# Attention steps of a two-layer decoder trunk in a fixed issue order on four engines

## The chip, the cores and the metric

One core of a Trainium2 chip runs the whole program. The metric is the device time of one execution in microseconds (us). Engine names are those of the profile: PE is TensorE (PEld its weight loads), DVE is VectorE, ACT is ScalarE, POOL is GpSimd, SP is SyncE, which issues nearly all DMAs.

## What is computed

The program is a decoder trunk of two layers on 512 tokens of width 1024, all in fp32. What matters here is the cross-attention of layer 1, a sliding window of 128 keys with ALiBi slopes and one sink logit per head:

```python
def mixer_b(xn, w_q, sinks, w_o, kblk, vblk):
    q = (xn @ w_q).reshape(B, nb, BLOCK, N_KV_HEADS, GQA_GROUP, HEAD_DIM)
    scores = jnp.einsum('bnikgd,bnjkd->bnkgij', q, kblk) * (HEAD_DIM ** -0.5)
    ...
    scores = scores - slopes[:, :, None, None] * dist
    scores = jnp.where(valid[None, :, None, None], scores, -jnp.inf)
    m = jnp.maximum(jnp.max(scores, axis=-1, keepdims=True), sink)
    e = jnp.exp(scores - m)
    probs = e / (jnp.sum(e, axis=-1, keepdims=True) + jnp.exp(sink - m))
    out = jnp.einsum('bnkgij,bnjkd->bnikgd', probs, vblk)
    return out.reshape(B, S, N_Q_HEADS * HEAD_DIM) @ w_o
```

There are 16 heads in 4 groups that share keys and values, and 4 blocks of 128 tokens. Around it stand norms, gated MLPs and dense products, which the change leaves alone.

## The kernel before, in words

Every fp32 product is made of three matmuls in a faster format (L191): weights and inputs are split into a high part (a cast) and a low part (the difference). A weight "unit" of 128x1024 is loaded by SP into one of a few raw buffers (`load`), cast by ACT into `wh` (L170) and subtracted by DVE into `wl` (L171); `pump` does this for the next units, `take` and `chunk` hand them to the matmuls. In the attention only two raw buffers are in use, so a load waits until the `wl` of the unit two before is done.

The attention runs 16 steps, one for each pair of group g and block n (i = 4g + n). A step i works on three attention blocks at different ages:

- `scores(i)`, L707: eight PE matmuls into the two PSUM banks `sc`.
- `logits(i)`: DVE merges the two key blocks (L720, not for n = 0), scales and adds ALiBi into `prs` (L721), for n = 0 masks instead (L723), and takes the row minimum `low` (L728).
- `exps(i)`, L736: four ACT exponentials, one a head, whose sums go to `sm`.
- `weights(i)`: DVE's reciprocal of `sm` (L742), then POOL multiplies `prs` by it (L743).
- `turn(i-1)`, L750: four PE transposes of the step before into the single PSUM bank `tr`; `turned_hi` casts it on ACT (L765, `ph` or `pp`), `turned_lo` takes the low part on DVE (L771) and POOL masks both (L774).
- `mix(i-2)`, L788: PE's product with the values into the single PSUM bank `pv`; `low_rows` copies half of it on ACT (L794, `pb`); `outputs` adds the halves on DVE (L806), casts on ACT (L810, `oh`) and subtracts on POOL (L813, `ol`).

Between these, PE does "fill" work, five pieces of three 512-column matmuls a step: 48 pieces of `project` (the queries of groups 1 to 3) and then pieces of `merge` (the output projection). A finished query half goes through `queries` (a cast on ACT, L259, a subtraction on DVE, L260, four DMAs of SP, about 0.6 us of issue each). A finished merge is added to h on DVE (L687). After every fourth step DVE rescales `alibi` (L726).

The order of the instructions on each engine is not the order of the code: a scheduler of the framework chooses it when the program is built, within the data dependencies. Each engine then runs its list strictly in that order.

Of the kernel before, what the change touches and what calls it, by code (L numbers as in the profile page):

```python
# [1 line left out]

# [50 lines left out]
def tile_yoco(ctx: ExitStack, tc: tile.TileContext, t, out: bass.AP, out_b: bass.AP):  # L53
# [18 lines left out]
    def psum2(name):  # L72
        return mmp.tile([P, 2, S], F32, tag="sc", name=name)


    units = []

# [257 lines left out]
    def slope(hd):  # L335
        return 2.0 ** (-8.0 * (hd + 1) / HEADS)
# [317 lines left out]
    for c in range(NC):  # L654
        ps = psum(f"vv{c}")
        mm3t(ps[:, :256], xkv, parts, 0, 256, c)
        vf.append(tp.tile([P, 256], F32, tag="rstd", name=f"vf{c}"))
        nc.scalar.activation(vf[c], ps[:, :256], AF.Copy, scale=rt[:, c : c + 1])
        halves(vt[c // 2][:, c % 2], vf[c])
        if c:  # L660
            d = tp.tile([P, 256], F32, tag="acc", name=f"vdf{c}")
            nc.gpsimd.tensor_sub(d, vf[c - 1], vf[c])
            halves(vd[:, c - 1], d)

    box = {}
# [12 lines left out]
    def merge(m, k0, k1, first, last, ps=None):  # L678

        c, half = m // 2, k0 // 4  # L680
        if (c, half) not in box:
            box[c, half] = chunk(256, 4, ahead=0)
        if first:
            box[f"o{m}"] = psum(f"o{m}_{half}", "mm") if ps is None else ps
        mm3(box[f"o{m}"], box[c, half][k0 % 4 : (k1 - 1) % 4 + 1], o2[k0:k1], m % 2 * P, first=first, last=last)
        if last:
            nc.vector.tensor_add(h[m], h[m], box[f"o{m}"])  # L687

    steps = [(g, n) for g in range(GROUPS) for n in range(NC)]
    live = {}  # L690
# [23 lines left out]
    def logits(i, o):  # L714

        g, n = steps[i]
        pr = prs[:, i % 2]
        cur = o[:, :, P:]
        if n:
            nc.vector.copy_predicated(cur, above.bitcast(U32).unsqueeze(1).to_broadcast([P, GQ, P]), o[:, :, :P])  # L720
        nc.vector.scalar_tensor_tensor(pr[:, :, :P], cur, rq[:, n : n + 1], alibi, op0=ALU.mult, op1=ALU.add)  # L721
# [3 lines left out]
        if n == NC - 1 and g + 1 < GROUPS:  # L725
            nc.vector.tensor_scalar_mul(alibi, alibi, slope(GQ - 1))  # L726
        low = at.tile([P, GQ], F32, tag="low", bufs=2, name=f"low{i}")
        nc.vector.tensor_reduce(low, pr, axis=mybir.AxisListType.X, op=ALU.min)  # L728
        sm = at.tile([P, GQ], F32, tag="sm", bufs=2, name=f"sm{i}")
        live[i] = [pr, low, sm]  # L730

    def exps(i, es):

        pr, low, sm = live[i]
        for e in es:
            nc.scalar.activation(pr[:, e, :], pr[:, e, :], AF.Exp, bias=low[:, e : e + 1], scale=-1.0,  # L736
                                 accum_out=sm[:, e : e + 1])

    def weights(i):

        pr, low, sm = live[i]
        nc.vector.reciprocal(sm, sm)  # L742
        nc.gpsimd.tensor_mul(pr[:, :, :P], pr[:, :, :P], sm.unsqueeze(2).to_broadcast([P, GQ, P]))  # L743

    def turn(i):
# [20 lines left out]

    def turned_lo(i, tr):

        n = steps[i][1]
        ph, pl, mh, ml = live[i]  # L770
        nc.vector.tensor_sub(pl, tr, ph.bitcast(F32))  # L771
        if n:
            for a, b in ((ph, mh), (pl, ml)):
                nc.gpsimd.affine_select(out=b, in_=a.bitcast(F32), pattern=[[0, GQ], [-1, P]], compare_op=ALU.is_gt,  # L774
                                        fill=0.0, base=0, channel_multiplier=1)

    def mix(i):

# [18 lines left out]
    def outputs(i, ps, b):  # L797

        g, n = steps[i]
        if n == 0:  # L800
            for m in (2 * g, 2 * g + 1):
                o2.append([ap.tile([P, S], F32R, tag=f"a{x}{m}", name=f"o{x}{m}") for x in "hl"])
        x, y = (a.rearrange("p (b e t) -> p b e t", b=2, e=2) for a in (ps, b))
        of = y[:, :, 0, :]
        for e in range(2):
            nc.vector.tensor_add(of[sides[e]], x[:HD, :, e, :], y[:HD, :, e, :])  # L806
        cols = slice(n * P, (n + 1) * P)
        for a in range(2):
            oh, ol = o2[2 * g + a]
            nc.scalar.copy(oh[:, cols], of[:, a, :])  # L810
        for a in range(2):
            oh, ol = o2[2 * g + a]
            (nc.gpsimd if i < last - 1 else nc.vector).tensor_sub(ol[:, cols], of[:, a, :], oh[:, cols].bitcast(F32))  # L813

    last = len(steps)
    work = [(project, u) for u in range(48)]
# [12 lines left out]
    sinks(0)  # L829
    for i in range(last):  # L830
        o = scores(i)
        logits(i, o)
        pump(state["next"] + WBUFS - 1)
        fill(i, 0, 3)
        if i:
            tr = turn(i - 1)
        exps(i, (0,))
        if i:
            turned_hi(i - 1, tr)
        exps(i, (1,))  # L840
        fill(i, 3, 4)
        if i >= 2:
            pv = mix(i - 2)
            pb = low_rows(i - 2, pv)
        exps(i, (2, 3))
        if i:
            turned_lo(i - 1, tr)
        if i >= 2:
            outputs(i - 2, pv, pb)
        fill(i, 4, None)  # L850
        weights(i)
        if i + 1 < last:
            sinks(i + 1)
    fill(last, 0, 2)
    tr = turn(last - 1)
    turned_hi(last - 1, tr)
    turned_lo(last - 1, tr)
    pv = mix(last - 2)
    outputs(last - 2, pv, low_rows(last - 2, pv))
    state["cap"] = len(units)  # L860
    load(held_back + 2)
    for m in (2, 3):
        merge(m, 4, 6, False, False)
    pv = mix(last - 1)
    outputs(last - 1, pv, low_rows(last - 1, pv))
    state["tags"], state["turn"] = list(range(RAWS)), 2
    load(held_back + 6)
    two = psum2("o5")
    merge(4, 4, 6, True, False, psum("o4_1", "tr"))
    merge(5, 4, 6, True, False, two[:, 0])  # L870
    piece, pef, pet = ple_in_both()
    nf = Norm("nf1", [(xp, "x", gain("norm_ffn", 1))])
    for m in range(KD):
# [209 lines left out]
```

## Time and profile before

| | us |
|---|---|
| median of three runs | 1145.34 |
| lowest and highest of them | 1145.27, 1147.95 |
| profiled execution, whole | 1146.59 |
| profiled execution, span from first to last instruction | 1144.9 |
| PE busy in the span | 1123.8 |
| PE waits between 593 and 701 us of the span | 5.9 |

The granted clock was 0.997 on average. A row of the timeline gives start and duration of an instruction, its engine and line, output<-inputs by the program's names, and in brackets how long the engine had sat idle and what ended that. In the tables of waits a row gives who waited for whom, the total, the number of times and the longest.

### The profile page before, as it was taken

The page shows a single profiled execution, that of the slowest core. Times are in us where ns is not written, and L with a number is a line of the kernel's source. Part 1 is how long each engine was busy: PE and PEld are TensorE (multiplying, and loading weights), DVE is VectorE, ACT ScalarE, POOL GpSimd, SP SyncE. Part 2 cuts the span into 40 slices and gives each one's busy share as a digit, 9 for nine tenths or more (in the row PEclk, how much of TensorE's full clock was granted, in tenths as well). Part 3 has the DMA queues.
Part 4 walks back from the last instruction along what each step waited for, and adds up shares of the span by engine and source line. Part 5 has one row for each costly group of instructions (what it writes and reads, how often), then busy time and mean ns, then how long its engine had stood idle before and what let it go on. Part 6 is the DMA issues. An engine that isn't in the chain of part 4 may idle for free.

```text
span 1144.9 us, 13730 instructions
## 1 busy us (share of the span) xinstructions
PE 1123.8 (98%) x5248; PEld 936.6 (82%) x5248; DVE 737.1 (64%) x983; ACT 509.7 (45%) x807; POOL 139.8 (12%) x169
## 2 busy tenths in 40 slices
PE   9999999999999999999998999999999999999996
PEld 7888888888888888888887778888888888888895
DVE  7356477763676367557867886687734774577656
ACT  6534344431343244445656666554423442344532
POOL 2100310000000000022225553200000000000232
PEclk9999999999999999999999999999999999999998
DMA  9322222322322333233063414433322323332202
GB/s 334 105 85 84 100 92 93 110 92 92 111 71 95 111 110 94 91 110 104 13 180 92 129 57 139 141 109 91 110 92 93 101 69 106 110 97 87 79 15 74
DMA packets 44690, 116.48 MB, mean 102 GB/s; under 512 B 4936, under 2 KB 16848, under 8 KB 44624
## 3 DMA queue, kind: packets, MB, share of 16 engines
q1 hardware_dynamic: 43504, 114.42, 31.8%
q10 hardware_dynamic: 1120, 1.18, 0.3%
q8 instruction: 41, 0.67, 0.2%
q14 instruction: 25, 0.20, 0.1%
HBM read 108.24 MB, written 2.11 MB: 96 GB/s over the span
## 4 chain that ended last, share of the span: by engine, by line
PE 89%; DVE 4%; ACT 2%; issue 2%; POOL 1%; DMA 1%; SPq 0%; POOLq 0%; ACTq 0%; DVEq 0%
PE up L197 14%; PE up L198 14%; PE up L199 14%; PE d L197 8%; PE d L199 8%; PE d L198 8%; PE gate L197 2%; PE gate L199 2%; PE gate L198 2%; PE u L199 1%; PE u L197 1%; PE u L198 1%; PE v L209 1%; PE v L208 1%; PE v L210 1%
## 5 line engine op out<-in xcount | busy, mean ns | idle before, releaser
L171 DVE TENSOR_TENSOR wl<-wraw,wh 128x1024 fp32r<-128x1024 f32 (+2 forms) x197 | 238.3, 1211 | 121.7 <-ACT wh L170 120.7
L170 ACT CAST wh<-wraw 128x1024 fp32r<-128x1024 f32 (+1 forms) x196 | 202.1, 1033 | 237.4 <-PE d L198 135.8
L197 PE MATMUL up<-nf00h,wh 128*128 128x512 f32 x352 | 137.1, 390 | 0.0
L197 PE MATMUL up<-nf10h,wh 128*128 128x512 f32 x352 | 137.0, 389 | 0.0
L199 PE MATMUL up<-nf00h,wl 128*128 128x512 f32 x352 | 137.0, 389 | 0.0
L199 PE MATMUL up<-nf10h,wl 128*128 128x512 f32 x352 | 136.9, 389 | 0.0
L198 PE MATMUL up<-nf10l,wh 128*128 128x512 f32 x352 | 136.9, 389 | 0.0
L198 PE MATMUL up<-nf00l,wh 128*128 128x512 f32 x352 | 136.9, 389 | 0.0
L197 PE MATMUL d<-ah,wh 128*128 128x512 f32 x352 | 136.9, 389 | 0.0
L198 PE MATMUL d<-al,wh 128*128 128x512 f32 x352 | 136.9, 389 | 0.0
L199 PE MATMUL d<-ah,wl 128*128 128x512 f32 x352 | 136.9, 389 | 0.0
L384 ACT ACTIVATE c<-hs,vec 128x512 f32<-128x512 f32 x88 | 71.7, 815 | 88.2 <-DVE hs L380 87.2
L385 DVE SCALAR_TENSOR_TENSOR c<-hs,vec,c 128x511 f32<-128x511 f32 x88 | 65.9, 749 | 37.4 <-ACT c L384 37.2
L358 DVE TENSOR_TENSOR h<-h,d 128x512 f32<-128x512 f32 x56 | 38.5, 687 | 69.0 <-PE d L199 69.0
L259 ACT CAST ah<-a 128x512 fp32r<-128x512 f32 x44 | 27.4, 622 | 113.5 <-DVE a L390 113.5
L199 PEld LDWEIGHTS up<-nf00h,wl 128*128 128x128 f32 x352 | 66.1, 188 | 13.9
L197 PEld LDWEIGHTS up<-nf10h,wh 128*128 128x128 f32 x352 | 66.1, 188 | 13.8
L199 PEld LDWEIGHTS d<-ah,wl 128*128 128x128 f32 x352 | 66.1, 188 | 13.8
L197 PEld LDWEIGHTS d<-ah,wh 128*128 128x128 f32 x352 | 66.1, 188 | 13.7
L198 PEld LDWEIGHTS up<-nf10l,wh 128*128 128x128 f32 x352 | 66.1, 188 | 13.7
L198 PEld LDWEIGHTS d<-al,wh 128*128 128x128 f32 x352 | 66.1, 188 | 13.7
L198 PEld LDWEIGHTS up<-nf00l,wh 128*128 128x128 f32 x352 | 66.1, 188 | 13.6
(314 smaller groups left out, 2031.1 us busy)
## 6 DMA issues: line engine op xcount, KB each, us to landing
wraw<-in_w_up SPq DMA_DIRECT2D x88, 512.0 KB, 3.5
wraw<-in_w_down SPq DMA_DIRECT2D x32, 512.0 KB, 3.6
wraw<-in_w_down SPq DMA_DIRECT2D x16, 384.0 KB, 3.2
wraw<-in_w_u SPq DMA_DIRECT2D x8, 512.0 KB, 5.7
wraw<-in_w_out SPq DMA_DIRECT2D x8, 512.0 KB, 3.5
wraw<-in_w_gate SPq DMA_DIRECT2D x8, 512.0 KB, 4.1
wraw<-in_w_q SPq DMA_DIRECT2D x8, 512.0 KB, 3.7
wraw<-in_w_o SPq DMA_DIRECT2D x8, 512.0 KB, 3.3
```

The source lines that it names most:

```text
L170: nc.scalar.copy(wh[:, :n], src)
L171: nc.vector.tensor_sub(wl[:, :n], src, wh[:, :n].bitcast(F32))
L197: nc.tensor.matmul(ps, wh[:, a:b], xh, start=st, stop=False)
L198: nc.tensor.matmul(ps, wh[:, a:b], xl, start=False, stop=False)
L199: nc.tensor.matmul(ps, wl[:, a:b], xh, start=False, stop=en)
L208: nc.tensor.matmul(ps, xh[:, s], wh[:, a:b], start=st, stop=False)
L209: nc.tensor.matmul(ps, xl[:, s], wh[:, a:b], start=False, stop=False)
L210: nc.tensor.matmul(ps, xh[:, s], wl[:, a:b], start=False, stop=en)
L259: nc.scalar.copy(hi, src)
L358: nc.vector.tensor_add(h[m], h[m], ps)
L384: nc.scalar.activation(c, hs, AF.Identity, bias=v("conv_b", l * 2 * NJ + col), scale=cw[2])
L385: nc.vector.scalar_tensor_tensor(c[:, 1:], hs[:, : S - 1], cw[1], c[:, 1:], op0=ALU.mult, op1=ALU.add)
```

## The change

1. A context `in_order` ties each instruction of PE, DVE, ACT and POOL inside it to the one before on the same engine, in the order of the code. The scheduler can no longer move them. SP is not tied.
2. The code of a step is put in a new order. The ACT copy `low_rows(i-2)` now comes after all four exponentials of step i, and the DVE additions of `outputs` for the same block come at the start of step i+1, ahead of `logits(i+1)`. The reciprocal is split from `weights`, which opens the next step on POOL. The query splits and the additions to h wait in `held` until `settle`.
3. Weight units are split one at a time, in the steps listed in `pumped`, before the exponentials of the step; raw loads are issued at the end of a step.
4. `values(3)` moves behind `scores(0)`, step 0 takes seven fill pieces instead of five, and the last fill pieces and the tail behind step 15 are rearranged.
5. One exponential of a single column right after the last gate of layer 0 brings the ACT table load there.

```diff
+    def in_order(*engines):
+        traced = nc.cur_bb.bb.instructions
+        n0 = len(traced)
+        yield
+        before = {}
+        for i in traced[n0:]:
+            e = i.engine
+            if e in engines:
+                if e in before:
+                    tc.add_manual_dep(i, before[e].name, ...)
+                before[e] = i
...
     ple(0, npl, nm, pe)
+    tc.keep_in_program_order(nc.scalar.activation(const.tile([P, 1], F32, name="warm_exp"), one, AF.Exp))
...
-    parts = chunk(256, KD)
+    vparts = chunk(256, KD, ahead=2)
...
-            queries(box["qp"], g, j)
+            held.append((queries, box["qp"], g, j))
...
+    def inverse(i):
+        nc.vector.reciprocal(live[i][2], live[i][2])
...
-    beside = [work[5 * i : 5 * i + 5] for i in range(last)]
-    beside.append([(merge, m, 4, 6, False, False) for m in (0, 1)])
+    work += [part(0, 4), part(1, 4)]
+    beside = [work[:7]] + [work[5 * i + 2 : 5 * i + 7] for i in range(1, last)]
+    pumped = (0, 1, 3, 4, 6, 7, 9, 10, 11, 13, 15)
...
-    pump(state["next"] + WBUFS)
+    pump(state["next"] + 2)
     sinks(0)
-    for i in range(last):
-        o = scores(i)
-        logits(i, o)
-        pump(state["next"] + WBUFS - 1)
-        fill(i, 0, 3)
-        if i:
-            tr = turn(i - 1)
-        exps(i, (0,))
-        if i:
-            turned_hi(i - 1, tr)
-        exps(i, (1,))
-        fill(i, 3, 4)
-        if i >= 2:
-            pv = mix(i - 2)
-            pb = low_rows(i - 2, pv)
-        exps(i, (2, 3))
-        if i:
-            turned_lo(i - 1, tr)
-        if i >= 2:
-            outputs(i - 2, pv, pb)
-        fill(i, 4, None)
-        weights(i)
-        if i + 1 < last:
-            sinks(i + 1)
+    with in_order(*engines):
+        for i in range(last):
+            o = scores(i)
+            if i >= 1:
+                weights(i - 1)
+            if i >= 3:
+                pairs = outputs(i - 3, *done.pop(i - 3))
+            logits(i, o)
+            if i >= 3:
+                output_lows(pairs, nc.gpsimd)
+            if i == 0:
+                values(3)
+            if i in pumped:
+                pump(state["unit"] + 1)
+            fill(i, 0, 3)
+            if i:
+                tr = turn(i - 1)
+            if i + 1 < last:
+                sinks(i + 1)
+            exps(i, (0, 1))
+            if i:
+                turned_hi(i - 1, tr)
+            exps(i, (2, 3))
+            if i:
+                masks(i - 1, (0,))
+                turned_lo(i - 1, tr)
+                masks(i - 1, (1,))
+            fill(i, 3, 4)
+            settle()
+            if i >= 2:
+                pv = mix(i - 2)
+            fill(i, 4, None)
+            inverse(i)
+            if i % NC == NC - 1 and i + 1 < last:
+                nc.vector.tensor_scalar_mul(alibi, alibi, slope(GQ - 1))
+            if i >= 2:
+                done[i - 2] = pv, low_rows(i - 2, pv)
+            load(min(state["unit"] + 2, held_back))
```

What stands in a row on DVE from the merge of step 5's scores to that of step 6's (`wl116` is a weight unit, `pl4` the low part of block 4, `pb3` the additions of block 3), before:

```order
L720 COPY_PREDICATED sc5_4965<-above_467,sc5_4965 128x4x128
L721 SCALAR_TENSOR_TENSOR prs_4630<-sc5_4965,rq_4380,alibi_4489 128x4x128
L742 RECIPROCAL sm4_4895<-sm4_4895 128x4
L728 TENSOR_REDUCE low5_4976<-prs_4630 128x4
L171 TENSOR_TENSOR wl116_4905<-wraw116_4902,wh116_4904 128x1024
L771 TENSOR_TENSOR pl4_4995<-tr4_4988,ph4_4994 128x512
L806 TENSOR_TENSOR pb3_5006<-pv3_5001,pb3_5006 64x2x128 x2
L742 RECIPROCAL sm5_4978<-sm5_4978 128x4
L720 COPY_PREDICATED sc6_5023<-above_467,sc6_5023 128x4x128
```

And of the change:

```order
L744 COPY_PREDICATED sc5_4964<-above_467,sc5_4964 128x4x128
L745 SCALAR_TENSOR_TENSOR prs_4587<-sc5_4964,rq_4382,alibi_4491 128x4x128
L750 TENSOR_REDUCE low5_4980<-prs_4587 128x4
L795 TENSOR_TENSOR pl4_5003<-tr4_4994,ph4_5002 128x512
L763 RECIPROCAL sm5_4982<-sm5_4982 128x4
L834 TENSOR_TENSOR pb3_5020<-pv3_5011,pb3_5020 64x2x128 x2
L744 COPY_PREDICATED sc6_5022<-above_467,sc6_5022 128x4x128
```

The weight unit has left this step, and the additions of `pb3` still stand ahead of the next merge, now behind the reciprocal.

On ACT the same step, from its exponentials (`sm5`) on, before:

```order
L736 ACTIVATE prs_4630,sm5_4978<-prs_4630,low5_4976 128x129 x2
L765 CAST ph4_4994<-tr4_4988 128x512
L794 COPY pb3_5006<-pv3_5001 64x512
L736 ACTIVATE prs_4630,sm5_4978<-prs_4630,low5_4976 128x129 x2
L810 CAST oh0_4793<-pb3_5006 128x128
```

And of the change:

```order
L758 ACTIVATE prs_4587,sm5_4982<-prs_4587,low5_4980 128x129 x2
L790 CAST ph4_5002<-tr4_4994 128x512
L758 ACTIVATE prs_4587,sm5_4982<-prs_4587,low5_4980 128x129 x2
L822 COPY pb3_5020<-pv3_5011 64x512
L838 CAST oh0_4825<-pb3_5020 128x128
```

The copy `pb3`, for which DVE's additions wait, has moved behind the last two exponentials.

The tail on ACT behind step 15's exponentials (`wh124` and `own123` are the weights of the next stage), of the change:

```order
L822 COPY pb13_5708<-pv13_5699 64x512
L838 CAST oh6_5652<-pb13_5708 128x128
L838 CAST oh7_5654<-pb13_5708 128x128
L822 COPY pb14_5728<-pv14_5723 64x512
L185 CAST wh124_5818<-wraw124_5768 128x1024
L790 CAST pp15_5741<-tr15_5736 128x512
L185 CAST own123_m4_5798<-wraw123_5766 128x1024
```

Before, `wh124` stood behind `pb13`, ahead of `oh6`, `oh7` and `pp15`, and `pb14` behind `own123`. The unit `wraw124` could be loaded a step earlier there, since `wl122` was made in step 14; in the change it is made in step 15.

More of the change, by code (lines that the diff above doesn't have):

```diff
@@ L663, in tile_yoco @@
             halves(vd[:, c - 1], d)
+    for c in range(3):
+        values(c)
     box = {}
@@ L807, in outputs, with output_lows @@
         cols = slice(n * P, (n + 1) * P)
[L808 to L813, printed above, removed]
+        pairs = [(of[:, a, :], *(x[:, cols] for x in o2[2 * g + a])) for a in range(2)]
+        for src, oh, ol in pairs:
+            nc.scalar.copy(oh, src)
+        return pairs
+    def output_lows(pairs, eng):
+        for src, oh, ol in pairs:
+            eng.tensor_sub(ol, src, oh.bitcast(F32))
     last = len(steps)
+    held = []
     work = [(project, u) for u in range(48)]
@@ L854, in tile_yoco, with settle @@
[L854 to L859, printed above, removed]
+    def settle():
+        for f, *args in held:
+            f(*args)
+        held.clear()
+    pump(state["next"] + 2)
+    sinks(0)
+    engines = [mybir.EngineType.PE, mybir.EngineType.DVE, mybir.EngineType.Activation, mybir.EngineType.Pool]
+    done = {}
+    with in_order(*engines):
[36 more added lines that the diff above has]
+            load(min(state["unit"] + 2, held_back))
+        settle()
+        weights(last - 1)
+        output_lows(outputs(last - 3, *done.pop(last - 3)), nc.gpsimd)
+        for m in (0, 1):
+            merge(m, 5, 6, False, False)
+        pv = mix(last - 2)
+        done[last - 2] = pv, low_rows(last - 2, pv)
+        merge(2, 4, 6, False, False)
+        tr = turn(last - 1)
+        turned_hi(last - 1, tr)
+        masks(last - 1, (0,))
+        turned_lo(last - 1, tr)
+        masks(last - 1, (1,))
+        output_lows(outputs(last - 2, *done.pop(last - 2)), nc.gpsimd)
@@ L860, in tile_yoco @@
+    two = psum2("o4")
+    merge(3, 4, 6, False, False)
+    merge(4, 4, 6, True, False, two[:, 0])
     state["cap"] = len(units)
     load(held_back + 2)
[L862 to L863 removed]
     pv = mix(last - 1)
[L865 removed]
+    output_lows(outputs(last - 1, pv, low_rows(last - 1, pv)), nc.vector)
     state["tags"], state["turn"] = list(range(RAWS)), 2
     load(held_back + 6)
[L868 to L869 removed]
@@ L870, in tile_yoco @@
-    merge(5, 4, 6, True, False, two[:, 0])
+    merge(5, 4, 6, True, False, psum("o5_1", "tr"))
     piece, pef, pet = ple_in_both()
```

29 lines of the change are left out of this document (17 added, 12 removed).

## Prediction

> **What bounds the kernel now.** The page's list of engines comes first, then PE's waits between 593 and 701 us, where the attention's 16 steps lie, then the windows.
>
> ```profile
> PE 1123.8 (98%) x5248; PEld 936.6 (82%) x5248; DVE 737.1 (64%) x983; ACT 509.7 (45%) x807; POOL 139.8 (12%) x169
> PE tr L750 <- POOL prs L743: 3.7, 6, 1.1
> PE sc L707 <- DMA q<-ql: 1.6, 1, 1.6
> PE o L198 <- POOL ol L813: 0.4, 1, 0.4
> PE pv L788 <- DVE pb L806: 0.2, 1, 0.2
> 599.46:685.36 85.90, 80.18 (x426) 66.17 (x425) 69.56 (x121) 58.04 (x187) 43.38 (x72) 1.00 0.33 90
> 685.36:701.77 16.41, 16.24 (x80) 13.13 (x80) 9.34 (x17) 8.44 (x23) 7.93 (x12) 1.00 0.50 157
> ```
>
> PE is the bound nearly everywhere, so a rearrangement can win only what PE waits: 5.9 us in the attention, mostly transposes `tr` that wait for POOL's weights `prs`. The first window runs from the merge of step 1's scores (599.46) to that of step 15's (685.36): 85.90 us for 14 steps, 6.14 a step. What does PE itself need? Two of its rows, the third score matmuls of steps 13 and 14, with no wait of PE between them:
>
> ```profile
> 671.75 0.28 PE L707 MATMUL sc<-kh,q 128*128 128x256 f32 x1
> 677.55 0.28 PE L707 MATMUL sc<-kh,q 128*128 128x256 f32 x1
> ```
>
> That is 5.80 us a step, and less where the mixed block has n = 0, with two `pv` matmuls fewer. So the question for the new order is whether DVE, ACT and POOL deliver a step every 5.8 us.
>
> **The chain of a step in the new order.** There it is serial, by the order lists: DVE merge, scale, minimum; ACT two exponentials, the cast of `tr`, two exponentials, the copy `pb`; DVE two additions; the next merge. The old order let two exponentials follow the copy. Step 15 of before happens to have run nearly the new sequence, with all four exponentials ahead of the copy, so the price can be read off:
>
> ```profile
> 684.38 0.85 DVE L806 TENSOR_TENSOR pb<-pv,pb 64x256 f32<-64x256 f32 x2 [0.31 <-ACT pb L794]
> 685.36 0.67 DVE L720 COPY_PREDICATED sc<-above,sc 128x512 f32<-128x512 uint32 x1
> 686.92 0.69 DVE L728 TENSOR_REDUCE low<-prs 128x4 f32<-128x516 f32 x1
> 687.70 0.41 ACT L736 ACTIVATE prs<-prs,low 128x129 f32<-128x129 f32 x1 [1.89 <-DVE low L728]
> 688.22 0.59 ACT L765 CAST ph<-tr 128x512 fp32r<-128x512 f32 x1
> 690.01 0.18 DVE L742 RECIPROCAL sm<-sm 128x4 f32<-128x4 f32 x1 [0.47 <-ACT prs L736]
> 690.00 0.58 ACT L794 COPY pb<-pv 64x512 f32<-64x512 f32 x1
> 690.62 0.85 DVE L806 TENSOR_TENSOR pb<-pv,pb 64x256 f32<-64x256 f32 x2 [0.43 <-ACT pb L794]
> ```
>
> Merge to additions took 5.26 (685.36 to 690.62); 0.12 of it is the cast's late `tr`. Additions to the next merge took 0.98 (684.38 to 685.36), of which 0.09 is a reciprocal that the new order has earlier. So 5.26 - 0.12 + 0.98 - 0.09 = **6.03 us a step**, over PE's 5.80. No engine's load does that, but the serial hand-overs: DVE was busy 69.56 of 85.90.
>
> A step with n = 0 has the masking copy in place of the merge; the next rows, which also carry the start, give 1.63 from scale to minimum against 1.56 from merge to minimum: 6.10.
>
> ```profile
> 597.23 0.74 DVE L721 SCALAR_TENSOR_TENSOR prs<-sc,rq,alibi 128x512 f32<-128x512 f32 x1
> 598.86 0.69 DVE L728 TENSOR_REDUCE low<-prs 128x4 f32<-128x516 f32 x1
> 590.54 0.28 PE L208 MATMUL vv<-wh,n10h 128*128 128x256 f32 x1
> 593.42 0.22 PE L707 MATMUL sc<-kh,q 128*128 128x128 f32 x1
> 594.26 0.44 PE L197 MATMUL q<-n11h,wh 128*128 128x512 f32 x1
> 597.53 0.39 PE L199 MATMUL q<-n11h,wl 128*128 128x512 f32 x1
> 598.03 0.39 PE L707 MATMUL sc<-kh,q 128*128 128x256 f32 x1
> 599.09 0.39 PE L197 MATMUL q<-n11h,wh 128*128 128x512 f32 x1
> ```
>
> **Extras on the chain.** These rows price them:
>
> ```profile
> 652.66 0.68 DVE L260 TENSOR_TENSOR ql<-q,qh 128x512 fp32r<-128x512 f32 x1
> 653.26 0.68 DVE L771 TENSOR_TENSOR pl<-tr,ph 128x512 fp32r<-128x512 f32 x1
> L171 DVE TENSOR_TENSOR wl<-wraw,wh x12: 1214/1226/1556, 593.5 to 691.6; 128x1024 fp32r<-128x1024 f32 x12
> L726 DVE TENSOR_SCALAR alibi<-alibi x3: 428/689/853, 613.0 to 663.9; 128x512 f32<-128x512 f32 x3
> 663.75 0.68 POOL L774 TENSOR_SCALAR_AFFINE_SELECT pm<-ph 128x512 fp32r<-128x512 f32 x1 [0.90 <-ACT ph L765]
> 663.85 0.85 DVE L726 TENSOR_SCALAR alibi<-alibi 128x512 f32<-128x512 f32 x1
> ```
>
> The queries' cast `qh` now stands behind the exponentials, and its subtraction ahead of the reciprocal: 0.59 as the cast at 688.22, 0.04 to hand over as from `pb` to the additions, 0.60 for the subtraction (652.66 to 653.26) and 0.09 for the reciprocal = 1.32, where the plain step has 0.62 for the copy (690.00 to 690.62). So +0.70, in steps 2, 4, 6, 7 and 9: 3.5 us. In step 1 no additions follow, so it takes the chain to the reciprocal and 0.09: 690.00 - 685.36 - 0.12 = 4.52, + 1.32 = 5.84.
>
> `alibi` now stands between reciprocal and additions, as the POOL mask ends. Its cost lies between 0.43, hidden in a plain step, and 0.85, the row beside a mask; I take the latter's side: 0.26 in step 3, 0.6 in step 7 behind the queries, and 0.7 in step 11 behind an addition to h. The two additions to h in step 10 (0.60 each, as `ql`) pass the copy by 0.5. Together 2.1, bounds 1.1 to 2.3.
>
> A weight unit's `wl` costs nothing: it follows the minimum (0.69) and takes 1.23, while DVE would sit idle until the low part of `tr`, 2.2 behind the minimum's start (0.78 to the first exponential, two of 0.40, the cast's 0.59). The longest `wl`, 1.56, would use that cover up; what goes beyond delays the additions only past another 0.6. Its cast on ACT lies beside merge, scale and minimum. The loads wait for a `wl` two units back, a step or more earlier, and landed in 3.1 to 7.2 us (row further down), so no query DMA is stuck behind them on SP. The table load costs nothing between two casts at the gate, where ACT sat idle 2.62 us:
>
> ```profile
> 596.87 1.28 ACT L736 ACT_TABLE_LOAD   x1
> 570.72 1.05 ACT L170 CAST wh<-wraw 128x1024 fp32r<-128x1024 f32 x1 [2.62 <-PE k L198]
> ```
>
> Nor does it win there: the first exponential waited for `low` (598.86 + 0.69) after the load had ended. Bounds 0 to 1.28.
>
> So from step 1's merge to step 15's: 5.84 + 10 x 6.03 + 3 x 6.10 + 3.5 + 2.1 = 90.0 against 85.90, **+4.1**. The old stalls on `q<-ql` and `tr` are in the 85.90 and do go, but the chain takes their place: PE waits for `prs` again, a little in almost every step.
>
> A rule of the Trainium skill speaks to `alibi`: SBUF — State Buffer, section "Who interferes with whom", says that a DVE instruction in a two-port mode (tensor_scalar can be one) and a GpSimd instruction shut each other out, whichever begins first holding the ports to its end. By it the row at 663.85, 0.10 behind a mask of 0.68, would be 0.58 + 0.43 = 1.01; it took 0.85, so the trace agrees in kind, not in full. With 1.01 in all three steps the term would be +4.6 in place of +4.1.
>
> **The start.** Scores 0 begin at 590.54 in place of the fourth value block: 0.84 (593.42 to 594.26), then the values 2.88, then 21 fill matmuls for 15 at 0.23 (594.26 to 597.53 is 14), 4.9, then 1.0 for scores 1: step 1's merge at 600.16 for 599.46, **+0.7**, with 1.4 us of fill work done ahead. Bounds 0.3 to 1.2.
>
> **The tail.** Count from step 15's merge, called c, to the first merge matmul of the next stage at 701.77: 16.41 before.
>
> ```profile
> L743 POOL TENSOR_TENSOR prs<-prs,sm x16: 1041/1042/1046, 601.8 to 690.3; 128x512 f32<-128x512 f32 x16
> 686.62 0.66 PE L750 MATMUL tr<-ident,prs 128*128 128x128 f32 x4
> 687.03 0.47 PE L197 MATMUL o<-oh,wh 128*128 128x512 f32 x1
> wraw<-in_w_pin SPq DMA_DIRECT2D x2, 512.0 KB, 4.1
> DMA to landing us min/median/max: 3.1/3.6/7.2
> 692.84 0.59 ACT L765 CAST pp<-tr 128x512 fp32r<-128x512 f32 x1 [0.79 <-PE tr L750]
> 693.32 1.05 ACT L170 CAST own_m<-wraw 128x1024 fp32r<-128x1024 f32 x1
> ```
>
> Transposes 14 start at c + 0.2: the reciprocal of step 14 is at c - 1.5 (4.53 behind its merge, of 6.03), POOL is then in the second mask of block 13 until about c - 0.9 (cast from 3.15 to 3.74, low part 0.69, mask 0.68, behind that merge), and the weights take 1.04. By the new list PE then has 0.41, 29 matmuls (6.7), transposes 15 and 9 matmuls (2.5), and stands at c + 9.8 at the next stage's first piece, which needs `own`. On ACT `own` stands behind `wh124`, whose raw tile can be loaded only after `wl122`, made in step 15 (done at c + 3.4). With 4.1 us to land it is there at c + 7.6; 1.05 for `wh124`, 0.48 (692.84 to 693.32) for `pp15`, 1.05 for `own`: c + 10.2, a wait of 0.4. Then 10 matmuls at 0.23, the piece's 12 half ones at half that, and some 0.6 of my estimate for waiting on `own`'s low part and the last `ol`, both queued behind `pp15`: c + 14.5. **-1.9** against before; bounds -2.5 (all on time) to +0.7.
>
> **Sum.** 0.7 + 4.1 - 1.9 = +2.9. The profiled execution took 1146.59 (span 1144.9 and 1.7 around it), so 1149.5; it lies 1.25 over the median, so **1148.2** for the median of runs. The terms' bounds give +0.9 to +6.2 if all fell on one side; for the chain case I take +1 to +5.2, 1146.3 to 1150.5.
>
> **Rivals.**
>
> *Late landing, clearly slower.* Place: `wh124` on ACT. Each us that unit 124 lands after c + 7.2 costs PE one, since `pp15` and `own` queue behind it. The total passes +3.4 from a landing time of 4.6 us. For it: 7.2 is the longest load shown, and unit 127 is in flight beside it. Against: 4.1 and 3.6 are usual. With 6 us, c + 9.5: 1.9 more, +4.8, 1150.1.
>
> *PE-bound after all.* If the hand-overs cost less than step 15's rows show, or the additions don't hold the merge, PE runs at its 5.80 and all 5.9 us of waits go: 1139.4. For it: DVE and ACT have the time in sum, and the late query DMA (1.6) goes surely, being issued a step earlier. Against: 6.03 is read off in one piece, in PSUM-bound instructions whose durations hardly vary (weights 1041 to 1046).
>
> *Nothing moves.* That the order isn't kept is excluded by the lists.
>
> **How the numbers follow.** About 0.3% (3.4 us) is what a measurement here can tell from no change. The chain as bound: 0.77, +1 to +5.2, of which 0.47 lies under +3.4 and 0.30 over it. Late landing: 0.13, all over. PE-bound: 0.10. So faster 0.10, same 0.47, slower 0.43. The range leaves out the PE-bound case and the far end of the late landing: 1144.8 to 1151.5.
>
> **What would show it.** Right: merge to merge 6.0 in plain steps (5, 13, 14), 6.7 in steps with queries, DVE waiting for `pb` in each; PE waiting for `prs` in most steps, and no longer for `q<-ql`; step 15's merge some 5 us later; PE waiting about half a us at `own`. Wrong: scores every 5.8 or less, and PE's waits under 2 us in all; or a wait on ACT ahead of an exponential, for a raw tile, which I have put at nothing.

## The result, and the profile after

The changed kernel took **1150.65 us** (median of ten runs, 1148.85 to 1151.36); the kernel before, run beside it, took 1146.73 (ten runs, 1145.27 to 1148.94). The ratio is **1.0033, interval 1.0023 to 1.0042**: slower by 3.9 us, with 1148.2 forecast and a range to 1151.5. The profiled execution took 1150.4, its span is 1148.7 where before's was 1144.9: +3.8.

First the page's list of engines, then PE's and DVE's waits from 590 to 710 us, then three windows: step 1's merge to step 15's, the tail up to the next stage's first merge matmul, and the next stage.

```profile
PE 1125.6 (98%) x5248; PEld 938.3 (82%) x5248; DVE 734.6 (64%) x983; ACT 509.8 (44%) x808; POOL 136.0 (12%) x169
```
```profile
PE tr L775 <- POOL prs L768: 4.2, 6, 1.3
PE o L212 <- ACT oh L838: 2.9, 1, 2.9
PE pv L816 <- DVE pb L834: 0.9, 1, 0.9
```
```profile
DVE pp L795 <- ACT pp L790: 8.9, 7, 1.9
DVE pl L795 <- ACT ph L790: 4.4, 8, 1.6
...
DVE pb L834 <- ACT pb L822: 3.2, 6, 1.0
```
```profile
600.51:690.49 89.98, 83.11 (x431) 68.05 (x429) 68.64 (x119) 55.23 (x177) 39.34 (x71) 0.98 0.31 92
690.49:705.73 15.24, 13.99 (x69) 11.38 (x69) 9.60 (x17) 9.38 (x24) 7.27 (x12) 1.00 0.38 122
705.73:1098.80 393.07, 393.07 (x1792) 327.80 (x1792) 254.70 (x315) 165.60 (x213) 20.33 (x14) 1.00 0.32 101
```

PE's wait for `q<-ql` is gone, as forecast, and its waits sum to 8.0 us in place of 5.9. But the loss isn't that sum. The account by place is: start +1.05 (600.51 for 599.46), the 14 steps +4.08 (89.98 for 85.90), tail -1.17 (15.24 for 16.41); together +3.96, against 3.8 in the span. Of the +4.08 only 1.15 is idle time of PE (85.90 - 80.18 = 5.72 before, 89.98 - 83.11 = 6.87 now). The other 2.93 is its busy time, which holds five matmuls more (431 for 426) and the stretch at half clock told of below.

The plain step runs as the prediction read it off. DVE's and ACT's rows of step 14:

```profile
684.45 0.68 DVE L744 COPY_PREDICATED sc<-above,sc 128x512 f32<-128x512 uint32 x1
686.09 0.69 DVE L750 TENSOR_REDUCE low<-prs 128x4 f32<-128x516 f32 x1
688.34 0.69 DVE L795 TENSOR_TENSOR pp<-tr,pp 128x512 fp32r<-128x512 f32 x1 [1.56 <-ACT pp L790]
...
689.72 0.85 DVE L834 TENSOR_TENSOR pb<-pv,pb 64x256 f32<-64x256 f32 x2 [0.43 <-ACT pb L822]
690.49 0.68 DVE L744 COPY_PREDICATED sc<-above,sc 128x512 f32<-128x512 uint32 x1
```
```profile
686.81 0.40 ACT L758 ACTIVATE prs<-prs,low 128x129 f32<-128x129 f32 x1 [1.70 <-DVE low L750]
687.72 0.59 ACT L790 CAST pp<-tr 128x512 fp32r<-128x512 f32 x1
688.60 0.39 ACT L758 ACTIVATE prs<-prs,low 128x129 f32<-128x129 f32 x1
689.10 0.58 ACT L822 COPY pb<-pv 64x512 f32<-64x512 f32 x1
```

Read them as one line of hand-overs: ACT waits 1.70 for DVE's minimum, DVE 1.56 for ACT's cast and 0.43 for the copy, then the additions, then the merge. Each engine is idle in turn and the step takes 6.04.

Step 10 does not fit. It took 8.03 (merges at 657.93 and 665.96), where the prediction had 6.5. PE's and ACT's rows show a wait that the prediction lacks, and windows laid on the trace's clock records show what followed (behind the length and the busy times of PE, PEld, DVE, ACT, POOL comes the granted clock):

```profile
658.45 0.79 PE L212 MATMUL o<-oh,wh 128*128 128x512 f32 x1 [2.86 <-ACT oh L838]
660.43 0.63 PE L213 MATMUL o<-ol,wh 128*128 128x512 f32 x1
662.07 0.60 PE L775 MATMUL tr<-ident,prs 128*128 128x128 f32 x4
```
```profile
662.71 0.59 ACT L790 CAST pp<-tr 128x512 fp32r<-128x512 f32 x1 [1.53 <-PE tr L775]
```
```profile
654.66:658.07 3.41, 0.93 (x8) 0.72 (x7) 2.41 (x7) 2.39 (x7) 0.62 (x1) 1.00 0.56 178
658.07:661.48 3.41, 3.03 (x7) 2.30 (x8) 3.12 (x4) 2.33 (x7) 1.41 (x4) 0.50 0.54 130
661.48:664.90 3.42, 3.42 (x21) 2.90 (x20) 1.57 (x3) 1.95 (x6) 1.27 (x2) 1.00 0.49 158
```

The fill piece that opens step 10 needs the output of block 7, group 1's last. Its additions now stand at the start of step 10 itself, so PE waited 2.86 us for `oh`. For the next 3.41 us PE had half its clock: matmuls of 0.63 start 0.43 apart, where they start 0.23 apart at full clock. The transposes came late for that, ACT waited 1.53 us for them in the middle of its exponentials, and the step grew.

### The profile page after: what moved, and what is told of

Same layout as the page of the kernel before. It is cut to its first block, busy times and chain, and to the rows that moved or that the text cites. A ratio compares the mean times of both kernels' runs of the same rounds, so it can differ in the third digit from the quotient of the medians.

```text
span 1148.7 us, 13690 instructions
## 1 busy us (share of the span) xinstructions
PE 1125.6 (98%) x5248; PEld 938.3 (82%) x5248; DVE 734.6 (64%) x983; ACT 509.8 (44%) x808; POOL 136.0 (12%) x169
## 4 chain that ended last, share of the span: by engine, by line
PE 88%; DVE 5%; ACT 3%; issue 1%; POOL 1%; DMA 0%; SPq 0%; POOLq 0%; DVEq 0%; ACTq 0%
PE up L212 14%; PE up L213 14%; PE up L214 14%; PE d L212 8%; PE d L213 8%; PE d L214 8%; PE gate L212 2%; PE gate L213 2%; PE gate L214 2%; ACT prs L758 2%; PE u L214 1%; PE u L212 1%; PE u L213 1%; PE v L224 1%; PE v L223 1%; PE v L225 1%
```

## The experiments

**Theory 1**: the serial chain of DVE and ACT sets the step, because the additions wait for `pb` and the next merge stands behind the additions. Rivals: the load of an engine, PE or the transfers; the copy's late place alone; parts of the change other than the order. **Theory 2**: step 10's wait and half clock cost 1.5 us. **Theory 3**: PE's wait of 0.95 at the values product of block 14 costs that much in the tail.

"Chain" is the time from step 1's merge to step 15's; PE's waits are summed over 590 to 712 us.

| kernel | median, us | ratio to before [interval] | chain, us | PE's waits, us |
|---|---|---|---|---|
| changed kernel | 1150.65 | 1.0033 [1.0023, 1.0042] | 89.98 | 8.0 |
| copies on the chain | 1156.29 | 1.0081 [1.0065, 1.0098] | 96.17 | 12.4 |
| copies beside it | 1150.97 | 1.0030 [1.0016, 1.0045] | 90.37 | 8.0 |
| `pb` early | 1154.93 | 1.0070 [1.0055, 1.0086] | 94.51 | 11.0 |
| `pb` early, additions ahead of reciprocal | 1148.42 | 1.0009 [1.0000, 1.0018] | 88.11 | 4.9 |
| no ties | 1144.09 | 0.9978 [0.9968, 0.9987] | 82.15 | 3.8 |
| no early table load | 1150.31 | 1.0029 [1.0019, 1.0039] | 88.85 | 8.1 |
| later output pieces | 1149.25 | 1.0022 [1.0013, 1.0030] | 89.13 | 7.6 |
| block 14 in another bank | 1150.86 | 1.0033 [1.0021, 1.0046] | 90.00 | 7.8 |
| additions late, with `oh` | 1163.82 | 1.0146 [1.0129, 1.0163] | 99.64 | 15.4 |
| additions late, `oh` apart | 1147.82 | 1.0008 [0.9999, 1.0018] | 86.51 | 4.1 |
| three edits | 1143.75 | 0.9977 [0.9968, 0.9986] | 84.59 | 3.8 |
| three edits, three banks | 1140.31 | 0.9943 [0.9930, 0.9955] | 79.67 | 0.2 |

**The same load on and off the chain.** Two ACT copies of a table that nothing in the attention reads any more, once behind the last exponentials, once ahead of the first:

```diff
+            if i:
+                for _ in range(2):
+                    nc.scalar.copy(dist, dist)
             if i >= 2:
                 done[i - 2] = pv, low_rows(i - 2, pv)
```

> The changed kernel with two more ACT copies of 128x128 (two such casts take 0.50 us in its trace) in steps 1 to 15, behind the last exponentials and ahead of the copy pb; they compute nothing. Theory 1 (the additions wait for pb, the next merge for the additions): 0.40 to 0.50 us more in each of the 14 steps, step 1 to step 15 96 to 97 us in place of 90.0, 5.5 to 7 us slower than the changed kernel, ratio 1.008 to 1.0095. Rival (PE or the loads set the pace): within 1.5 us of the changed kernel.

> The same two copies, ahead of the first two exponentials, where ACT sat idle for 0.74 us or more before low: the same load on ACT, off the chain. Theory 1: no change, step 1 to step 15 in 89.5 to 90.7, within 1 us of the changed kernel. Rival (ACT's load, not the place, counts): as much slower as with the copies behind the exponentials.

The chain grew by 6.19 us with the copies on it (0.44 a step on average: 0.52 in the plain steps 13 and 14, nothing in step 1, 0.99 in step 10, where PE also had half its clock for twice as long) and by 0.39 with them beside it, all of it in step 10 (8.48 for 8.03); the times by 5.6 and 0.3. DVE's and ACT's rows with the copies on the chain, then ACT's with them off it:

```profile
695.65 0.85 DVE L834 TENSOR_TENSOR pb<-pv,pb 64x256 f32<-64x256 f32 x2 [0.95 <-ACT pb L822]
696.42 0.68 DVE L744 COPY_PREDICATED sc<-above,sc 128x512 f32<-128x512 uint32 x1
```
```profile
687.83 0.62 ACT L909 COPY dist<-dist 128x128 f32<-128x128 f32 x2
688.47 0.58 ACT L822 COPY pb<-pv 64x512 f32<-64x512 f32 x1
```
```profile
679.91 0.62 ACT L893 COPY dist<-dist 128x128 f32<-128x128 f32 x2
680.75 0.41 ACT L758 ACTIVATE prs<-prs,low 128x129 f32<-128x129 f32 x1 [0.22 <-DVE low L750]
```

DVE's wait for `pb` goes from 0.43 to 0.95 in the first; in the second the copies only shorten the time in which ACT waits for `low`. The place counts, not the load: theory 1 holds against every rival that goes by load.

**The copy `pb` early, additions where they are.**

```diff
             exps(i, (0, 1))
             if i:
                 turned_hi(i - 1, tr)
+            fill(i, 3, 4)
+            if i >= 2:
+                pv = mix(i - 2)
+                done[i - 2] = pv, low_rows(i - 2, pv)
             exps(i, (2, 3))
```

> Only the place of the copy pb on ACT changes: between the cast of tr and the last two exponentials; the additions stay behind the reciprocal, and the reciprocal waits for all four exponentials. Theory 1 (the serial chain of DVE and ACT sets the step, whatever the order inside it): the copy's 0.6 us now lies ahead of the last exponentials in place of behind them, the chain is as long as before, merge to merge stays at 6.0 in plain steps, and the time stays within 1 us of the changed kernel's (ratio to the kernel before 1.002 to 1.004). Rival (it is the copy's late place on ACT that costs, and the additions follow it): 0.6 us less in each of 14 steps, 8 us faster than the changed kernel (ratio 0.996).

Plain steps took 6.12 and 6.11 (13 and 14), so the rival falls: the copy's place alone gains nothing, because the reciprocal, which stands ahead of the additions, now waits for the later exponentials. But the time rose by 4.3 us, where theory 1 said under 1. The steps with queries grew by 0.6 to 0.76 each (steps 2, 4, 6, 7 and 9 took 7.24, 7.41, 7.32, 7.62 and 7.32): there the copy used to run beside the subtraction `ql`, and now it stands ahead of the cast `qh`. The chain's price depends on what runs beside what in every kind of step, and I had checked the plain one only.

**Additions ahead of the reciprocal.** As above, and:

```diff
+            if i >= 2:
+                of = sums(i - 2, pv, pb)      # the additions
             inverse(i)
+            settle()
+            if i >= 2:
+                pairs = highs(i - 2, of)      # the casts oh
```

> Copy pb between the exponentials, and the additions in the same step ahead of the reciprocal, the query subtraction behind it: the additions no longer stand between reciprocal and merge. Theory 1: the chain falls to merge 0.0, second exponentials done at 5.2, reciprocal, next merge at about 5.45, under PE's 5.66 to 5.8; PE sets the pace, step 1 to step 15 takes 81 to 84 us in place of 90.0. The output of block 7 is also there a step earlier, so that PE's 2.86 us wait for oh in step 10 goes. 6 to 9 us faster than the changed kernel, ratio to the kernel before 0.995 to 0.998. Rival (PE or the loads bound the changed kernel already, the chain only follows): within 2 us of the changed kernel.

The plain step fell to 5.46, as worked out (5.45). Its rows, DVE first:

```profile
682.91 0.67 DVE L744 COPY_PREDICATED sc<-above,sc 128x512 f32<-128x512 uint32 x1
...
687.40 0.85 DVE L838 TENSOR_TENSOR pb<-pv,pb 64x256 f32<-64x256 f32 x2
688.27 0.18 DVE L763 RECIPROCAL sm<-sm 128x4 f32<-128x4 f32 x1
688.37 0.67 DVE L744 COPY_PREDICATED sc<-above,sc 128x512 f32<-128x512 uint32 x1
```

The additions now run beside the last exponentials and the reciprocal is followed by the merge at once. But the whole gained 2.2 us, not 6 to 9. Query steps still took 6.42 to 6.55 (step 7, with `alibi`, 7.02), since the query subtraction still stands ahead of the next merge, and steps 10 and 11 took 8.80 and 7.17: PE waited 0.91 for `oh` and 0.60 for `ol` at step 10's first piece, which is still too early, the clock halved again (below), and the additions to h behind the reciprocal lie on the chain.

**No ties.**

```diff
-    with in_order(*engines):
+    with in_order():
```

> The changed kernel's code without the ties: the framework's scheduler orders the engines again. In the steps from 6 on the list of DVE then has the next merge ahead of the additions, and the ACT list the cast of tr ahead of all four exponentials. Theory 1 (the fixed place of the additions ahead of the merge is the price of the order): 2 to 5 us faster than the changed kernel, plain steps under 5.8, ratio 0.9985 to 1.0015. Rival (the other parts of the change make the loss, not the order): within 1 us of the changed kernel or slower, with the scheduler's own waits back.

This takes back the order and keeps the rest, and the result is **faster than both**: 6.6 us under the changed kernel, 2.8 under the kernel before. So the rest of the change, in the scheduler's order, gains a little, and the fixed order costs more than that. The sign was right, the size more than I said, and the reason in part another. ACT's rows of step 13:

```profile
673.31 0.59 ACT L790 CAST ph<-tr 128x512 fp32r<-128x512 f32 x1 [0.63 <-PE tr L775]
674.37 0.41 ACT L758 ACTIVATE prs<-prs,low 128x129 f32<-128x129 f32 x1 [0.48 <-DVE low L750]
676.05 0.58 ACT L822 COPY pb<-pv 64x512 f32<-64x512 f32 x1
```

Copy, additions and merge still follow each other here (merges at 672.02 and 677.44: 5.42). What left the chain is the cast of `tr`: it runs while ACT would wait for `low` anyway, and the step is shorter by just its 0.6. In the changed kernel the same cast always stands between two exponentials. Only in steps 3, 6, 7, 11 and 15 did the scheduler put the merge ahead of the additions.

**Later output pieces (theory 2) and no early table load.**

```diff
-    work += [part(m, k) for m, k in ((4, 0), (4, 1), (5, 0), (5, 1), (4, 2), (4, 3), (5, 2), (5, 3))]
-    work += [part(m, k) for m in (6, 7, 0, 1, 2, 3) for k in range(4)]
+    work += [part(m, k) for k0 in (0, 2) for m in (4, 5, 6, 7) for k in (k0, k0 + 1)]
+    work += [part(m, k) for m in range(4) for k in range(4)]
...
-    pumped = (0, 1, 3, 4, 6, 7, 9, 10, 11, 13, 15)
+    pumped = (0, 1, 3, 4, 6, 7, 9, 10, 12, 13, 15)
```

> The pieces of the output projection that need block 7 of group 1 come four pieces or more later, one weight unit is split in step 12 in place of 11. Theory 2 (step 10's wait of PE for oh, 2.86 us, and the half clock behind it lengthen the chain by 1.5 us through the late transposes): step 10 falls from 8.03 to about 6.5, the time by 1.5 us, ratio 1.001 to 1.003. Rival (the chain of step 10 is long by itself, with two additions to h behind the exponentials, and PE only stands because it is ahead): step 10 stays above 7.5, no gain, ratio 1.0033.

1.4 us faster, and step 10 fell to 6.05 (the additions to h moved with the pieces, so that steps 11 and 12 took 6.95 and 6.60). There is no wait for `oh` and no half clock in its trace. Theory 2 holds for the two together. What each costs this run can't say, since it moves additions to h as well: the chain as a whole is only 0.85 shorter (89.13 for 89.98). The next run parts them.

```diff
-    tc.keep_in_program_order(nc.scalar.activation(const.tile([P, 1], F32, name="warm_exp"), one, AF.Exp))
```

> The changed kernel without the early exponential of one column: the table load goes back ahead of step 0's first exponential. Forecast of the prediction (the load costs nothing at either place): within 0.6 us of the changed kernel. Rival (the load, 1.28 us, is on the start's path there): 0.7 to 1.3 us slower, step 1's merge at 601.2 to 601.8 in place of 600.5.

The median differs by 0.3 us. Step 1's merge came at 600.73 for 600.51, within the scatter of the other runs whose start is the changed kernel's (600.02 to 601.39). So the load's place is worth nothing that these runs can tell, as the prediction had it. The trace shows something else, though: the same 2.86 us wait for `oh`, and no half clock behind it. PE's row, and the windows on this run's clock grid:

```profile
658.66 0.50 PE L212 MATMUL o<-oh,wh 128*128 128x512 f32 x1 [2.86 <-ACT oh L837]
```
```profile
653.98:657.39 3.41, 1.83 (x12) 1.46 (x10) 2.42 (x4) 3.26 (x11) 0.00 (x0) 1.00 0.37 131
657.39:660.80 3.41, 2.10 (x8) 1.53 (x9) 3.19 (x8) 1.74 (x4) 2.03 (x4) 1.00 0.70 177
```

The wait fell across two windows, with PE busy for 1.83 and 2.10 us of them; in the changed kernel's profiled run nearly all of it fell into one (busy 0.93). Step 10 took 6.88 here and 8.03 there, and ACT waited 0.39 for the transposes here and 1.53 there. So of the 1.5 us over the forecast 1.15 are the half clock and 0.35 what the wait costs without it. The chain, 88.85, is even a little shorter than with the later pieces (89.13): what those gained is mainly the clock.

**Block 14 in another bank (theory 3).**

```diff
-        pv = mix(last - 2)
+        two = psum2("o4")
+        pv = mix(last - 2, two[:, 1])
```

> The values product of block 14 goes to the other bank of sc in place of the single bank pv, so that PE needn't wait for the additions of block 13. Theory 3 (PE's wait of 0.95 us there is on the path): 0.5 to 0.95 us faster than the changed kernel, the first o<-oh of the next stage at c + 14.4 in place of c + 15.24. Rival (the wait moves to own or to the transposes of block 15): less than 0.3 us, with a wait at own or tr in its place.

No gain (1150.86): theory 3 falls and its rival holds. PE's wait at the additions went, and two others stood in its place at the next values product:

```profile
700.91 0.49 PE L816 MATMUL pv<-pp,vt 128*128 128x512 f32 x1 [0.47 <-ACT pp L790]
702.05 0.50 PE L816 MATMUL pv<-pm,vd 128*128 128x512 f32 x1 [0.65 <-POOL pm L802]
```

**Additions late instead of early.** The other way to take them from ahead of the merge, on top of the later pieces:

```diff
-            if i >= 3:
-                pairs = outputs(i - 3, *done.pop(i - 3))
             logits(i, o)
+            if i >= 3:
+                pairs = outputs(i - 3, *done.pop(i - 3))
```

> The kernel with the later output pieces (step 1 to step 15 in 89.1 us, 1149.25 us), and one thing more: the additions come behind the minimum of the next step in place of ahead of its merge; the copy pb stays behind the exponentials. Theory 1 (the additions, waiting for pb, hold up the merge): the next merge only waits for the scores and the reciprocal, about 4.8 us behind the last one, so PE sets the pace; step 1 to step 15 in 82 to 85 us, 4 to 7 us faster than with the later pieces alone, ratio to the kernel before 0.996 to 0.9985. PE may wait some 0.2 us a step for the bank pv. Rival (the wait only moves to that bank: the additions now end 3.1 us behind the merge, the values product wants the bank 1.6 behind it): less than 2 us faster.

A clear miss: 14.6 us slower than the later pieces alone. The edit moves more than the additions. `outputs` also issues the casts `oh`, which ACT now meets ahead of the exponentials; in the trace's sum of waits that is the largest:

```profile
ACT oh L838 <- DVE pb L834: 43.7, 14, 4.3
```

ACT waited there for the minimum and the additions behind it, with `wh` and the exponentials queued behind. So the next run put the casts behind the cast of `tr`:

```diff
             logits(i, o)
+            if i >= 3:
+                of = sums(i - 3, *done.pop(i - 3))
...
                 turned_hi(i - 1, tr)
+            if i >= 3:
+                output_lows(highs(i - 3, of), nc.gpsimd)
             exps(i, (2, 3))
```

> As the run with the additions behind the minimum, but without what that edit took along: its two ACT casts oh stood ahead of the next exponentials and waited there for the additions (wh and the exponentials behind them; steps of 5.96 to 8.5 us). Here the casts come between the cast of tr and the last two exponentials. Theory 1 (additions off the way between reciprocal and merge, and nothing put in their place): merge to merge 5.3 to 5.8 in plain steps, 6.0 in query steps, step 1 to step 15 in 82 to 86 us, 3 to 7 us faster than with the later output pieces alone (1149.25), ratio to the kernel before 0.996 to 0.9995. Rival (the bank pv, which the late additions hold, sets the pace instead): PE waits for it in most steps as in the last run (7.3 us), less than 2 us faster or slower.

1.4 us faster than the later pieces alone, less than the 2 us that separate the theories, so the rival holds. PE's sum, and DVE's rows:

```profile
PE pv L816 <- DVE pb L838: 3.6, 8, 0.8
```
```profile
681.66 0.70 DVE L744 COPY_PREDICATED sc<-above,sc 128x512 f32<-128x512 uint32 x1 [0.84 <-PE sc L731]
683.93 0.84 DVE L838 TENSOR_TENSOR pb<-pv,pb 64x256 f32<-64x256 f32 x2
```

The merge now waits for PE's scores, and PE for the bank `pv` until the additions, which stand behind that merge: a second loop, of 6.07 in step 13 (675.59 to 681.66) and 5.64 in step 14, whose values product is half as long. Of the three places tried for the additions, only the one ahead of the reciprocal brought plain steps under 5.5.

**The three edits together.** Additions ahead of the reciprocal, the later pieces, and `settle` (query subtractions, additions to h) behind the next minimum, where DVE sat idle for the cast:

```diff
             inverse(i)
-            settle()
+            if i == 2:
+                settle()
...
             logits(i, o)
+            settle()
```

> Three edits together: copy pb between the exponentials and additions ahead of the reciprocal; the output pieces that need block 7 later; and the query subtractions and the additions to h a step later, behind the minimum, where DVE sat idle for the cast of tr (only in step 2 they stay at the end, for the queries of group 1). Theory 1: no step over 6.0 but 3, 7 and 11 (alibi), PE at its own pace, step 1 to step 15 in 80.5 to 83.5 us, 6 to 9 us faster than the changed kernel, ratio 0.995 to 0.998: faster than the kernel before. Rival (what is taken off the chain comes back as PE waits for oh and as half clock): less than 3 us faster than the changed kernel.

6.9 us faster than the changed kernel and 3.2 faster than the kernel before, but the chain took 84.59, not 80.5 to 83.5: PE waited 1.65 and 2.22 us at two output pieces for a bank whose reader was now late, and the clock halved behind the second. Opening three banks ahead of block 7's pieces in place of four takes both away:

```diff
-    work += [part(m, k) for k0 in (0, 2) for m in (4, 5, 6, 7) for k in (k0, k0 + 1)]
-    work += [part(m, k) for m in range(4) for k in range(4)]
+    work += [part(m, k) for k0 in (0, 2) for m in (4, 5, 6) for k in (k0, k0 + 1)]
+    work += [part(m, k) for m in (7, 0, 1, 2, 3) for k in range(4)]
```

> The three edits together as before, with the output pieces in another order: three banks are opened ahead of block 7's pieces in place of four, so that PE needn't wait for a bank whose query subtraction or addition to h is now late (1.65 and 2.22 us in that run, the second with half clock behind it). Theory 1: both waits and the half clock go, step 1 to step 15 in 80.5 to 82.5 us, 2 to 3.5 us faster than the three edits before, ratio to the kernel before 0.9945 to 0.9965. Rival (PE waits elsewhere instead, for the outputs of block 7): within 1 us of the three edits before.

**1140.31 us, ratio 0.9943 [0.9930, 0.9955]**: 10.3 us under the changed kernel and 6.5 under the kernel before. The window of the 14 steps, and all that PE waited for:

```profile
600.77:680.44 79.67, 79.28 (x425) 66.35 (x424) 68.33 (x118) 55.29 (x178) 38.79 (x70) 1.00 0.36 104
```
```profile
PE tr L775 <- POOL prs L768: 0.2, 1, 0.2
```

PE was busy for 79.28 of 79.67 us. The fixed order keeps PE fed once the chain is shorter than PE's own step.

## Why the prediction came out as it did

**What bounds the kernel: right, and shown.** The chain of hand-overs takes PE's place; the copies on and beside it settle that. Plain steps were forecast at 6.03 and took 6.04, steps 8 and 12 (n = 0) at 6.10 and took 6.11 and 6.09. Two of the signs named came weaker than said: PE waited for `prs` six times, as often as before, not in most steps, and DVE for `pb` in steps 5, 8, 13, 14 and 15 only.

**The sum of the chain, 90.0 for 89.98: right only since two errors cancel.** By steps, measured against forecast:

| steps | forecast | measured | difference |
|---|---|---|---|
| 1 | 5.84 | 5.64 | -0.20 |
| 2, 4, 6, 9 (queries) | 27.0 | 26.27 | -0.7 |
| 7 (queries, `alibi`) | 7.33 | 7.01 | -0.32 |
| 3, 11 (`alibi`) | 13.02 | 12.71 | -0.3 |
| 10 | 6.53 | 8.03 | +1.50 |

The query term was mis-sized: step 9's rows show why (DVE's, then ACT's).

```profile
656.50 0.69 DVE L275 TENSOR_TENSOR ql<-q,qh 128x512 fp32r<-128x512 f32 x1 [0.56 <-ACT qh L274]
...
657.20 0.82 DVE L834 TENSOR_TENSOR pb<-pv,pb 64x256 f32<-64x256 f32 x2
657.93 0.68 DVE L744 COPY_PREDICATED sc<-above,sc 128x512 f32<-128x512 uint32 x1
```
```profile
655.51 0.39 ACT L758 ACTIVATE prs<-prs,low 128x129 f32<-128x129 f32 x1
655.90 0.57 ACT L274 CAST qh<-q 128x512 fp32r<-128x512 f32 x1
```

`qh` started 0.39 behind the last exponential, where `pb` starts 0.50 behind it in step 14, and the merge came 0.73 behind the additions' start in place of 0.77: +0.54 a step in place of 0.70. `alibi` took 0.80 once, in step 3, and 0.40 twice (three rows, 395/397/800 ns), where I had charged the long form in all three. The long one began at 617.40, 0.11 behind the start of a POOL mask of 0.63. In step 7 the mask had ended 0.54 before, and in step 11 it had 0.11 left. By the rule of the Trainium skill that the prediction cites (SBUF — State Buffer, "Who interferes with whom") the three would have taken 0.92, 0.40 and 0.51, an estimate from these rows; the trace, with 0.80, 0.40 and 0.40, agrees in kind, not in full.

The term that failed is step 10's: that the additions to h "pass the copy by 0.5" is all that the prediction adds there to a plain step, and the step ran 1.50 over it, 1.15 of that at half clock. The prediction counted what moved on DVE and ACT, but not that `outputs` of block 7, a step later, has a reader at the head of PE's list in that very step. The profile before gave the hint: PE's one wait for `ol`, of 0.4 us, fell into step 10 already (at 656.56).

**The start, +0.7 forecast, +1.05 measured**, inside its bounds: scores 0 began at 590.81 in place of 590.54. These are single traces, and with step 1's merge between 600.02 and 601.39 in the other runs with this start, the term isn't known to better than about half a us.

**The tail, -1.9 forecast, -1.17 measured.** The wait of 0.4 at `own` didn't occur: ACT cast `wh124` at 698.53 and `own` from 700.27 to 701.33 (c + 10.8, later than the c + 10.2 of the forecast), but PE came later too, its first matmul with `own` starting at 701.67. In place of that wait PE waited 0.95 for the bank `pv` at block 14, which the prediction missed. Taking the 0.95 away gained nothing: other waits stand right behind it, for block 15's `pp` and `pm`, so the bank alone is not the tail's bound.

**The terms put at nothing** hold: the table load (by experiment), and `wl`, `wh` and the raw loads (no wait on ACT ahead of an exponential but for `low`).

**The rivals.** Late landing didn't occur. PE-bound was put at 1139.4 and 0.10; the changed kernel is far from it, and the last experiment reached 1140.31 when the chain was cut. So the price of the waits in the profile before was about right, and this order didn't win it.

## What to carry to other kernels

When the order of several engines is fixed by hand, lay out the chain of hand-overs of each kind of step (with and without queries, with and without a unit to split) and compare it with the pace of the engine that should be the bound: here 6.04 against 5.7 us (79.67 for 14 steps in the last experiment) decided it, with DVE, the busiest of the others, busy for only 68.64 of 89.98 us. Then take whole pieces off the chain, by putting them where their engine waits anyway, and list each reader and each bank of what has moved: two of the misses here (`oh` at the head of step 10, `oh` ahead of the exponentials) were instructions that came along with the one that was meant. One added wait of PE may also cost its clock.

## What was not expected of the hardware

The granted clock changes on a fixed grid. In the changed kernel's trace it changes at 6.13, 658.08, 661.49 and 1142.77 us of the span: 191, 1 and 141 times 3.413 us apart. The window at half clock is just one period, and the one ahead of it is the one in which PE stood. That fits the Trainium skill, TensorE: Matmul & The Clock Gate, "Part 1: The HAM clock gate", which tells of a free-running activity window of 3413 ns. The same page ("HAM oscillation") warns of gaps over about 3.4 us; here a wait of 2.86 was enough when most of it lay in one window, and the same wait across two windows was not. Even less did it when the additions went ahead of the reciprocal, with 0.91 and 0.60 us of waiting:

```profile
653.96:657.37 3.41, 1.90 (x8) 1.27 (x8) 2.84 (x6) 2.08 (x6) 2.00 (x4) 1.00 0.64 193
657.37:660.78 3.41, 3.41 (x12) 2.73 (x11) 1.97 (x3) 1.47 (x5) 0.40 (x1) 0.50 0.53 132
```

PE was busy for 1.90 us there and lost its clock; in the run without the early table load it was busy for 1.83 and kept it. So the share of busy time alone doesn't decide, and what does stays open. The grid isn't tied to the program: the clock's first change came anywhere between 4.39 and 7.76 us into the span in the 14 traces. So the same kernel can pay or not pay from run to run, and the mean clocks of the single executions fit that. One window at half clock lowers the mean by about 0.0015 (half of 3.41 in 1148.7, an estimate). Of the changed kernel's ten executions the quickest, 1148.85 us, had a mean of 0.998, the other nine, 1150.40 to 1151.36, had 0.995 or 0.996. Without the early table load the three at 0.998 took 1148.81 to 1149.47 and the three at 0.994 or 0.995 took 1150.87 to 1151.22. So part of the spread of the times goes with the clock, and so does part of the changed kernel's loss: with the later pieces no execution was quicker than 1149.17, and the changed kernel at 0.998 was.
